# Two-input elementwise work moved to VectorE, small loads issued by GpSimd, conditioning chunks regrouped

## The chip, the cores and the metric

The kernel runs on one core of a Trainium2 chip. The metric is the device time of one execution in microseconds (us). Five engines work side by side, each with its own instruction queue that runs strictly in order: TensorE (PE in the profile) multiplies matrices, VectorE (DVE) and GpSimd (POOL) do elementwise work, ScalarE (ACT) applies functions of one input, SyncE (SP) issues most transfers. The transfers themselves run on 16 DMA engines. Semaphores tie the queues together.

## The reference

Two layers of a diffusion backbone work on 256 latent tokens and 256 context tokens of width 1024, in float32. Each layer first mixes tokens and then runs a mixture of experts:

```python
mod = silu(c) @ ada_w[l] + ada_b[l]          # 6 x 1024 values: shift, scale, gate, twice
h   = layer_norm(x) * (1 + scale) + shift
p   = h @ w_in                               # 1024 x 7328
branches = [mla(p), conformer_conv(p), fnet(p), rglru(p) * gelu(p)]
out = sum_k sigmoid(gate_k) * (branches[k] @ w_branch[k]) @ w_out
x   = layer_norm(alpha * x + gate * out)
x   = layer_norm(alpha * x + gate2 * expert_choice_moe(modulate(x)))
```

`rglru` is a gated linear recurrence in both directions. With r a sigmoid gate, log a = -8 softplus(-lambda) r, a = exp(log a), and the input is scaled by sqrt(1 - a^2). The conformer branch has a depthwise convolution with 31 taps. Layer 1 mixes only the latent tokens, with keys, values and recurrence states from the context.

## The kernel before

**Precision.** Products in the mixers are done with operands split in two parts: a high part, rounded by ScalarE (`S.activation(..., Copy)` into a 32-bit rounded type), and a low part, source minus high part (`lo_part`, line 148, one `tensor_tensor` subtraction). `mm3` (lines 151 to 153) then issues three matmuls: high by high, high by low, low by high. Every weight goes through `wsplit` (line 335), four 128 x 128 blocks at a time, into one of 4 (layer 0) or 5 (layer 1) pairs of buffers `wh`, `wl`. So each split costs one ScalarE and one subtraction, and TensorE can be some pairs ahead.

**Who subtracts.** `WSPLIT` deals the subtractions in turn: in layer 0 to GpSimd and VectorE alternately, in layer 1 three of five to GpSimd. GpSimd also has some other two-input operations: the square a*a of the recurrence (line 715), the sum of the two directions (line 734), the running sum over branches (line 496), and half of the low parts of `w_out` (line 1117).

**Order.** The mixer is written as code, and a scheduler in the language orders each engine's queue when the kernel is built. Convolution taps (line 525, 31 for each of four channel tiles, on VectorE) are queued in `later` and let out by `tick` four at a time (`PACE`) after each projection, so that they fill VectorE's gaps. The stages of a mixer are: four convolution inputs (glu), the Fourier branch, four recurrence tiles (`lru_in`, `lru_out`), attention; the gate and branch products of finished branches (`merge`) fill in between.

**Conditioning.** The 6144 columns of `ada_w` for each layer come in chunks. The first 2048 columns of layer 0 (shift and scale) are needed before anything else: `first_ada` loads eight chunks, each with 128 columns of shift and 128 of scale, as rows of 512 bytes. The other 27 chunks (384 columns, 1.5 MB each) sit in `ada_q`. `ada_more(AKEEP[l])` takes one at 24 places of a mixer while more than `AKEEP[l]` are left. A chunk takes a slot of the weight ring (three slots in the mixers), 8 small-output matmuls (`ada_mm`, line 208), one ScalarE copy, three transposes (line 218) and two small VectorE operations. With `AKEEP = (4, 0)`, 23 are done in layer 0's mixer, and the last four are loaded at its end (`AHELD`).

**Experts.** `finish` computes `w_out`, normalisation and routing, and then streams 16 experts' weights, 277 MB for each layer, through a ring.

Of the kernel before, what the change touches and what calls it, by code (L numbers as in the profile page):

```python
# [47 lines left out]
AKEEP = (4, 0)  # L48
AHELD = 4
WSPLIT = ("GV", "GGVGV")  # L50
# [49 lines left out]
def hybrid_kernel(ctx: ExitStack, tc: tile.TileContext, out: bass.AP, A):  # L100
# [102 lines left out]
    def ada_mm(l, pieces, w):  # L203
# [6 lines left out]
        part = adap[0].tile([128, 384], F32, name="adapart", tag="adapart", bufs=2)  # L210
        S.activation(out=part[:, 0:n], in_=ps[:, 0:n], func=AF.Copy)
        return l, pieces, part

    def ada_fin(l, pieces, part):
# [4 lines left out]
        red = const.tile([128, 3, 2], F32, name="adared", tag="adared", bufs=2)  # L219
# [53 lines left out]
    def params(l, rows):  # L273
# [29 lines left out]
        sp = const.tile([128, 4, 2, 2], F32, name="lsp", tag="lsp")  # L303
        V.tensor_tensor(out=p, in0=p, in1=mx, op=ALU.add)
        V.tensor_scalar(out=sp[:, :, :, 0], in0=p, scalar1=-4.0, scalar2=None, op0=ALU.mult)
        V.tensor_scalar(out=sp[:, :, :, 1], in0=p, scalar1=4.0, scalar2=None, op0=ALU.mult)
        prm[l, "sp"] = sp
# [10 lines left out]

    flip = [0]


    def mixer(l, tail=None):
# [12 lines left out]
        adap[0] = mixp  # L335
        def wsplit(v, k, m):
# [5 lines left out]
            flip[0] += 1  # L342
            lo_part(G if WSPLIT[l][flip[0] % len(WSPLIT[l])] == "G" else V, b, v, a)
# [9 lines left out]
        if both:  # L353
# [22 lines left out]
            params_load(0, rows, nc.scalar)  # L376
            parts = [ada_mm(*early.pop(0))]
            for j in range(KD):
                if j < 7:
                    parts.append(ada_mm(*(early.pop(0) if early else first_ada(j + 1))))  # L380
                ada_fin(*parts.pop(0))
# [20 lines left out]
        else:  # L402
# [4 lines left out]
            def front(t):  # L407
# [7 lines left out]
                for j0 in (0, 4):  # L415
# [12 lines left out]
                    lo_part(G if j0 else V, hl[:, j0:j0 + 4, c], hf[:, j0:j0 + 4], hh[:, j0:j0 + 4, c])  # L428
# [43 lines left out]
        def merge(b, br):  # L472
# [3 lines left out]
            for q in range(4):  # L476
# [7 lines left out]
                for i in range(2):  # L484
# [9 lines left out]
                    else:  # L494
                        V.scalar_tensor_tensor(out=sg, in0=sg, scalar=1.0, in1=pp[:, 0:N], op0=ALU.add, op1=ALU.mult)  # L495
                        G.tensor_tensor(out=merged[:, d, 0:N], in0=merged[:, d, 0:N], in1=sg, op=ALU.add)  # L496
# [78 lines left out]
        lo_part(G, dcl, dcf, dch)  # L575
        S.activation(out=dth, in_=dtf, func=AF.Copy)
        lo_part(G, dtl, dtf, dth)
# [84 lines left out]
        def lru_in(ct):  # L662
            bd = lp.tile([128, 2, 2, 128], F32, name="bd", bufs=nb2)
            G.memset(bd, 0.0)
            for ax, name in ((0, "lru_wa"), (1, "lru_wx")):
                for u in range(2):
                    nc.scalar.dma_start(out=bd[64 * u:64 * u + 64, :, ax, 64 * u:64 * u + 64],
                                        in_=A[name][l, :, 2 * ct + u].rearrange("d i j -> i d j"))
# [24 lines left out]
            lo_part(G, bl, bv, bh)  # L693
            return ge, xc, xh, xl, bh, bl

        def lru_out(ct, ge, xc, xh, xl, bh, bl):
# [13 lines left out]
            for d in range(2):  # L710
                a = lp.tile([128, 512], F32, name=f"a{d}", bufs=nb2)
                S.activation(out=a, in_=rr[d], func=AF.Exp, scale=sp[:, ct, d, 0:1], bias=sp[:, ct, d, 0:1])
                S.activation(out=rr[d], in_=rr[d], func=AF.Tanh, scale=sp[:, ct, d, 1:2], bias=sp[:, ct, d, 1:2])
                q = lp.tile([128, 512], F32, name="q2", bufs=2)
# [778 lines left out]
```

## Time and profile before

| what | value |
|---|---|
| median of 3 runs | 2454.8 us (2451.98 to 2458.52) |
| the profiled execution | 2450.92 us |
| its span in the trace | 2449.1 us |
| layer 0: mixer, then experts | about 0 to 620 us, then to 1362 us |
| layer 1: mixer, then experts | about 1362 to 1780 us, then to the end |

Times inside the trace are counted from the span's start; 1.8 us of the execution lie outside the span. An engine's busy time is the time in which at least one of its instructions runs; its share of a stretch says how full it was there, and the waits say who kept it from working. The granted clock is the share of TensorE's full speed in a stretch.

### The profile page before, as it was taken

The page shows a single profiled execution, that of the slowest core. Times are in us where ns is not written, and L with a number is a line of the kernel's source. Part 1 is how long each engine was busy: PE and PEld are TensorE (multiplying, and loading weights), DVE is VectorE, ACT ScalarE, POOL GpSimd, SP SyncE. Part 2 cuts the span into 40 slices and gives each one's busy share as a digit, 9 for nine tenths or more (in the row PEclk, how much of TensorE's full clock was granted, in tenths as well). Part 3 has the DMA queues.
Part 4 walks back from the last instruction along what each step waited for, and adds up shares of the span by engine and source line. Part 5 has one row for each costly group of instructions (what it writes and reads, how often), then busy time and mean ns, then how long its engine had stood idle before and what let it go on. Part 6 is the DMA issues. An engine that isn't in the chain of part 4 may idle for free.

```text
span 2449.1 us, 35574 instructions
## 1 busy us (share of the span) xinstructions
PE 2051.7 (84%) x14909; PEld 1212.6 (50%) x14909; DVE 983.3 (40%) x1811; ACT 632.4 (26%) x1162; POOL 394.8 (16%) x357
## 2 busy tenths in 40 slices
PE   6999999999879898898887788989967766767665
PEld 4876767757754343333332477778942211312111
DVE  5878844352671131121211688886551100100102
ACT  4354544452330010000000446656520000000000
POOL 1233322313300000000000155434600000000000
PEclk9999999999999999999999889999987666766658
DMA  9564444416579999999999443343699999999997
GB/s 273 163 183 148 155 119 138 135 34 230 166 288 395 423 420 422 423 423 423 423 423 423 148 119 116 87 139 104 222 375 423 423 423 424 423 423 423 424 423 302
DMA packets 238241, 713.11 MB, mean 291 GB/s; under 512 B 38183, under 2 KB 186137, under 8 KB 188928
## 3 DMA queue, kind: packets, MB, share of 16 engines
q1 hardware_dynamic: 227856, 703.37, 74.4%
q10 hardware_dynamic: 9072, 4.61, 0.7%
q8 instruction: 117, 1.92, 0.3%
q0 software_dynamic: 1152, 2.85, 0.3%
q14 instruction: 44, 0.36, 0.0%
HBM read 709.74 MB, written 1.05 MB: 290 GB/s over the span
## 4 chain that ended last, share of the span: by engine, by line
DMA 45%; PE 39%; DVE 7%; ACT 4%; issue 2%; POOL 1%; ACTq 0%; SPq 0%; DVEq 0%; POOLq 0%
DMA wslot<-in_w_e_down_dram 16%; DMA wslot<-in_w_e_up_dram 15%; DMA wslot<-in_w_e_gate_dram 13%; PE mm L151 6%; PE mm L153 6%; PE mm L152 6%; PE p L1348 3%; PE py L1386 2%; PE pp L153 2%; PE pp L151 2%; PE pp L152 2%; PE ax L208 2%; PE sc L909 1%; DVE conv L525 1%; PE xp L1229 1%
## 5 line engine op out<-in xcount | busy, mean ns | idle before, releaser
L1348 PE MATMUL p<-wslot,xe 128*32 128x352 f32 x6144 | 613.5, 544 | 164.4 <-DMA wslot<-in_w_e_gate_dram 94.5
L1348 PEld LDWEIGHTS p<-wslot,xe 128*32 128x32 f32 x6144 | 203.3, 122 | 561.2 <-issue 261.0
L1386 PE MATMUL py<-wslot,ht 128*32 128x256 f32 (+2 forms) x2176 | 283.0, 492 | 82.2 <-DMA wslot<-in_w_e_down_dram 42.2
L151 PE MATMUL mm<-hh,wh 128*128 128x512 f32 (+2 forms) x864 | 310.6, 360 | 11.7 <-ACT wh L341 4.9
L153 PE MATMUL mm<-hh,wl 128*128 128x512 f32 (+2 forms) x864 | 304.2, 353 | 17.3 <-DVE wl L148 13.4
L152 PE MATMUL mm<-hl,wh 128*128 128x512 f32 (+2 forms) x864 | 303.6, 352 | 0.4 <-DVE hl L148 0.4
L1361 DVE TENSOR_TENSOR he<-he,p 128x352 f32<-128x352 f32 x48 | 24.3, 507 | 683.1 <-PE p L1348 683.1
L148 POOL TENSOR_TENSOR wl<-wslot,wh 128x512 fp32r<-128x512 f32 (+1 forms) x163 | 225.4, 1389 | 417.8 <-ACT wh L341 394.0
L1360 ACT ACTIVATE he<-p 128x352 f32<-128x352 f32 x48 | 22.3, 464 | 964.7 <-PE p L1348 962.8
L341 ACT ACTIVATE wh<-wslot 128x512 fp32r<-128x512 f32 (+1 forms) x296 | 180.7, 624 | 288.6 <-PE mm L152 165.0
L1386 PEld LDWEIGHTS py<-wslot,ht 128*32 128x32 f32 (+1 forms) x2176 | 110.0, 130 | 248.7 <-issue 89.9
L1393 DVE SCALAR_TENSOR_TENSOR yt<-py,wix,gate 32x512 f32<-32x512 f32 (+1 forms) x128 | 78.6, 614 | 299.3 <-PE py L1386 297.8
L525 DVE SCALAR_TENSOR_TENSOR conv<-up,prm,conv 128x512 f32<-128x512 f32 (+1 forms) x240 | 194.2, 817 | 3.5
L151 PEld LDWEIGHTS mm<-hh,wh 128*128 128x128 f32 (+1 forms) x864 | 166.3, 193 | 49.0 <-issue 12.1
L153 PEld LDWEIGHTS mm<-hh,wl 128*128 128x128 f32 (+1 forms) x864 | 166.5, 193 | 43.1 <-DVE wl L148 15.7
L152 PEld LDWEIGHTS mm<-hl,wh 128*128 128x128 f32 (+1 forms) x864 | 166.7, 193 | 24.0 <-issue 3.1
L148 DVE TENSOR_TENSOR wl<-wslot,wh 128x512 fp32r<-128x512 f32 x133 | 109.5, 823 | 119.1 <-ACT wh L341 117.3
L153 PE MATMUL pp<-bh,wl 128*128 128x512 f32 (+1 forms) x256 | 87.2, 341 | 4.9 <-POOL wl L148 4.9
L151 PE MATMUL pp<-bh,wh 128*128 128x512 f32 (+1 forms) x256 | 87.3, 342 | 4.0 <-ACT bh L511 3.3
L152 PE MATMUL pp<-bl,wh 128*128 128x512 f32 (+1 forms) x256 | 86.7, 339 | 0.0
L1321 POOL DMA_DIRECT2D big<-in_ln_g_dram x1 | 0.6, 551 | 481.4 <-PE xp L1229 481.4
L496 POOL TENSOR_TENSOR big<-big,sg 128x512 f32<-128x512 f32 (+1 forms) x48 | 58.4, 1217 | 55.9 <-DVE sg L495 49.9
(367 smaller groups left out, 2569.9 us busy)
## 6 DMA issues: line engine op xcount, KB each, us to landing
wslot<-in_w_e_gate_dram SPq DMA_DIRECT2D x128, 1408.0 KB
wslot<-in_w_e_up_dram SPq DMA_DIRECT2D x128, 1408.0 KB
wslot<-in_w_e_down_dram SPq DMA_DIRECT2D x128, 1408.0 KB
wslot<-in_ada_w_dram SPq DMA_DIRECT2D x26, 1536.0 KB
wslot<-in_w_in_dram SPq DMA_DIRECT2D x36, 1024.0 KB
wslot<-in_w_branch_dram SPq DMA_DIRECT2D x32, 512.0 KB
wslot<-in_w_in_dram SPq DMA_DIRECT2D x30, 512.0 KB
wslot<-in_w_out_dram SPq DMA_DIRECT2D x12, 1024.0 KB
```

What stands on the lines that cost most here:

```text
L148: eng.tensor_tensor(out=lo, in0=src, in1=hi.bitcast(F32), op=ALU.subtract)
L151: T.matmul(o, lhsT=ah, rhs=bh, start=start, stop=False)
L152: T.matmul(o, lhsT=ah, rhs=bl, start=False, stop=False)
L153: T.matmul(o, lhsT=al, rhs=bh, start=False, stop=stop)
L208: T.matmul(ps[32 * g:32 * g + 32, 0:n], lhsT=csil[:, 2 * g + kk, :], rhs=w[:, 2 * g + kk, :], start=(kk == 0), stop=(kk == 1), skip_group_ ...
L341: S.activation(out=a, in_=v, func=AF.Copy)
L496: G.tensor_tensor(out=merged[:, d, 0:N], in0=merged[:, d, 0:N], in1=sg, op=ALU.add)
L525: V.scalar_tensor_tensor(out=cv, in0=up[:, :, k:k + 256], scalar=pm[:, ct, R_CVW + k:R_CVW + k + 1], in1=cv, op0=ALU.mult, op1=ALU.add)
L909: T.matmul(sc[:, 0:nk], lhsT=qt[:, q0:q0 + 128], rhs=kt[:, 0:nk], start=True, stop=True)
L1348: T.matmul(ts[si][32 * q:32 * q + 32, 0:FB], lhsT=xe[:, k, el, 32 * si:32 * si + 32], rhs=v[:, kk, FB * q:FB * q + FB], start=(k == 0), st ...
L1386: T.matmul(py[M * u:M * u + M, c:c + 256 * n], lhsT=ht[:, k], rhs=v[:, 256 * (i - 11 * kc):256 * (i - 11 * kc + n)], start=(k == 0), stop= ...
L1393: V.scalar_tensor_tensor(out=yt[s][32 * el:32 * el + 32, c], in0=py[ps_, 0:dw], scalar=wix[ps_, e:e + 1], in1=gate2[ps_, :], op0=ALU.mult, ...
```

## The change

Six edits go together.

1. `lo_part` runs on VectorE everywhere in the mixers and in `w_out`; so do the sum of the two directions and the running sum over branches. `WSPLIT` is gone.
2. The square of `a` becomes a second exponential on ScalarE, with twice the exponent (a third column of `sp`).
3. `params_load` of layer 0 (11 loads) and the block-diagonal gate weights `bd` (four loads for each of eight tiles) are issued by GpSimd instead of ScalarE; `bd` has one buffer in both layers.
4. The first eight conditioning chunks become four units of 256 shift and 256 scale columns, each loaded as two halves of the contraction, in rows of 1 KB (`first_ada`, `first_mm`); one unit serves two of the eight column tiles j.
5. `AKEEP` goes from (4, 0) to (11, 0): seven chunks pass from layer 0's mixer to layer 1's.
6. The inputs ctx and x are loaded as four transfers instead of two.

```diff
-AKEEP = (4, 0)
+AKEEP = (11, 0)
-WSPLIT = ("GV", "GGVGV")
...
+    def first_mm(u, pool):
+        ps = pax()
+        for half in range(2):
+            w = early.pop(0) if early else first_ada(2 * u + half)
+            for g in range(4):
+                T.matmul(ps[32 * g:32 * g + 32, :], lhsT=csil[:, 2 * g + half, :], rhs=w[:, g, :], start=(half == 0),
+                         stop=(half == 1), skip_group_check=True)
+        part = pool.tile([128, 512], F32, name="adafirst", bufs=2)
+        S.activation(out=part, in_=ps, func=AF.Copy)
+        return 0, [(256 * u, 256 * u + 256), (D + 256 * u, D + 256 * u + 256)], part
...
+        V.tensor_scalar(out=sp[:, :, :, 2], in0=p, scalar1=-8.0, scalar2=None, op0=ALU.mult)
...
-            flip[0] += 1
-            lo_part(G if WSPLIT[l][flip[0] % len(WSPLIT[l])] == "G" else V, b, v, a)
+            lo_part(V, b, v, a)
...
-            params_load(0, rows, nc.scalar)
-            parts = [ada_mm(*early.pop(0))]
+            params_load(0, rows, nc.gpsimd)
             for j in range(KD):
-                if j < 7:
-                    parts.append(ada_mm(*(early.pop(0) if early else first_ada(j + 1))))
-                ada_fin(*parts.pop(0))
+                if j % 2 == 0:
+                    ada_fin(*first_mm(j // 2, glp))
...
-                    lo_part(G if j0 else V, hl[:, j0:j0 + 4, c], hf[:, j0:j0 + 4], hh[:, j0:j0 + 4, c])
+                    lo_part(V, hl[:, j0:j0 + 4, c], hf[:, j0:j0 + 4], hh[:, j0:j0 + 4, c])
...
-                        G.tensor_tensor(out=merged[:, d, 0:N], in0=merged[:, d, 0:N], in1=sg, op=ALU.add)
+                        V.tensor_tensor(out=merged[:, d, 0:N], in0=merged[:, d, 0:N], in1=sg, op=ALU.add)
...
-            bd = lp.tile([128, 2, 2, 128], F32, name="bd", bufs=nb2)
+            bd = lp.tile([128, 2, 2, 128], F32, name="bd", bufs=1)
...
-                    nc.scalar.dma_start(out=bd[64 * u:64 * u + 64, :, ax, 64 * u:64 * u + 64],
+                    nc.gpsimd.dma_start(out=bd[64 * u:64 * u + 64, :, ax, 64 * u:64 * u + 64],
...
+                q = lp.tile([128, 512], F32, name="q2", bufs=2)
+                S.activation(out=q, in_=rr[d], func=AF.Exp, scale=sp[:, ct, d, 2:3], bias=sp[:, ct, d, 2:3])
                 S.activation(out=rr[d], in_=rr[d], func=AF.Tanh, scale=sp[:, ct, d, 1:2], bias=sp[:, ct, d, 1:2])
-                q = lp.tile([128, 512], F32, name="q2", bufs=2)
-                G.tensor_tensor(out=q, in0=a, in1=a, op=ALU.mult)
...
-            G.tensor_tensor(out=hs[0][:, t0:512], in0=hs[0][:, t0:512], in1=hs[1][:, t0:512], op=ALU.add)
+            V.tensor_tensor(out=hs[0][:, t0:512], in0=hs[0][:, t0:512], in1=hs[1][:, t0:512], op=ALU.add)
...
-                    lo_part(V if k0 else G, wl[:, k:k + 2, :], src, wh[:, k:k + 2, :])
+                    lo_part(V, wl[:, k:k + 2, :], src, wh[:, k:k + 2, :])
...
-    def first_ada(j):
-        return ada_load(0, [(128 * j, 128 * j + 128), (D + 128 * j, D + 128 * j + 128)])
+    def first_ada(i):
+        u, half = i // 2, i % 2
+        v = slot()[:, 0:2048].rearrange("p (g n) -> p g n", g=4)
+        for i in range(2):
+            c = i * D + 256 * u
+            nc.sync.dma_start(out=v[:, :, 256 * i:256 * i + 256],
+                              in_=A["ada_w"][0, :, c:c + 256].rearrange("(g h p) n -> h p g n", h=2, p=128)[half])
+        return v
```

The edits move instructions at three places that matter below.

TensorE at the start of layer 0, before (`ax` are the conditioning products, `adapart` their copy, `big` the normalised tokens, `mm` the first convolution input):

```order
L208 MATMUL ax<-wslot,csil 32x256 x24
L218 MATMUL tp<-c_ident,adapart 128x128 x2
L386 MATMUL tp<-c_ident,big 128x128 x4
L218 MATMUL tp<-c_ident,adapart 128x128 x2
L208 MATMUL ax<-wslot,csil 32x256
L386 MATMUL tp<-c_ident,big 128x128 x4
L208 MATMUL ax<-wslot,csil 32x256 x7
L218 MATMUL tp<-c_ident,adapart 128x128 x2
L151 MATMUL mm<-hh,wh 128x512
```

The same place in the change:

```order
L218 MATMUL ax<-wslot,csil 32x512 x8
L228 MATMUL tp<-c_ident,adafirst 128x128 x4
L393 MATMUL tp<-c_ident,big 128x128 x8
L218 MATMUL ax<-wslot,csil 32x512 x8
L228 MATMUL tp<-c_ident,adafirst 128x128 x4
L393 MATMUL tp<-c_ident,big 128x128 x8
L150 MATMUL mm<-hh,wh 128x512
L151 MATMUL mm<-hl,wh 128x512
```

Three eighths of the conditioning came before the first transposes of the tokens, one eighth at a time after; now it comes in quarters, and each quarter is followed by the transposes of two tiles instead of one.

VectorE at the end of `lru_out` of the first recurrence tile in layer 0, before (`q` is the scaled input, `r` holds the scans' results, `ge` the output, `wl` a weight's low part):

```order
L726 SCALAR_TENSOR_TENSOR r_1664<-a_1684,q_1687 128x512
L729 SCALAR_TENSOR_TENSOR r_1676<-a_1690,q_1693 128x256
L680 TENSOR_SCALAR xc<-xp,prm 128x512
L731 SCALAR_TENSOR_TENSOR r_1676<-a_1690,r_1676,q_1693 128x256
L683 SCALAR_TENSOR_TENSOR xc<-xp,prm,xc 128x512
L735 TENSOR_TENSOR ge<-ge,r_1664 128x512
L683 SCALAR_TENSOR_TENSOR xc<-xp,prm,xc 128x512
L148 TENSOR_TENSOR wl<-wslot,wh 128x512
L148 TENSOR_TENSOR bl<-ge,bh 128x512
```

The same place in the change:

```order
L736 SCALAR_TENSOR_TENSOR r_1615<-a_1629,q_1631 128x256
L687 TENSOR_SCALAR xc<-xp,prm 128x512
L738 SCALAR_TENSOR_TENSOR r_1615<-a_1629,r_1615,q_1631 128x256
L690 SCALAR_TENSOR_TENSOR xc<-xp,prm,xc 128x512
L741 TENSOR_TENSOR r_1603<-r_1603,r_1615 128x512
L690 SCALAR_TENSOR_TENSOR xc<-xp,prm,xc 128x512
L742 TENSOR_TENSOR ge<-ge,r_1603 128x512
L690 SCALAR_TENSOR_TENSOR xc<-xp,prm,xc 128x512
L231 TENSOR_REDUCE adared<-tp 128x6
L147 TENSOR_TENSOR bl<-ge,bh 128x512
L237 TENSOR_TENSOR mods_112<-adared,adab_108 128x6
L147 TENSOR_TENSOR wl<-wslot,wh 128x512 x2
```

The sum of the two scans (L741) now stands in VectorE's own queue, and the next low parts of weights stand behind it and behind the output `ge` and its low part `bl`, where before one stood ahead of `bl` and others were on GpSimd's queue.

SyncE's loads for layer 1's mixer from its first convolution input on, before:

```order
L134 DMA wslot<-in_w_in_dram 128x8x128 x8
L568 DMA wslot<-k_dftc_dram 128x256
L569 DMA wslot<-k_dftt_dram 128x2x256
L134 DMA wslot<-in_w_in_dram 128x8x256 x2
L134 DMA wslot<-in_w_in_dram 128x8x128 x4
L481 DMA wslot<-in_w_in_dram 128x8x256
```

The same place in the change:

```order
L133 DMA wslot<-in_w_in_dram 128x8x128 x4
L133 DMA wslot<-in_ada_w_dram 128x8x384
L133 DMA wslot<-in_w_in_dram 128x8x128 x2
L133 DMA wslot<-in_ada_w_dram 128x8x384
L133 DMA wslot<-in_w_in_dram 128x8x128 x2
L133 DMA wslot<-in_ada_w_dram 128x8x384
L575 DMA wslot<-k_dftc_dram 128x256
L576 DMA wslot<-k_dftt_dram 128x2x256
L133 DMA wslot<-in_w_in_dram 128x8x256 x2
L133 DMA wslot<-in_ada_w_dram 128x8x384 x2
L133 DMA wslot<-in_w_in_dram 128x8x128 x4
L488 DMA wslot<-in_w_in_dram 128x8x256
```

Five of the seven late conditioning chunks now stand between the convolution and Fourier weights, in the same three slots; the other two follow in the recurrence stage.

## Rows read from the trace of the kernel before

**Rows 1.** The page: the chain that ended last, by engine

```profile
DMA 45%; PE 39%; DVE 7%; ACT 4%; issue 2%; POOL 1%; ACTq 0%; SPq 0%; DVEq 0%; POOLq 0%
```

**Rows 2.** Windows by stage: stretch, length, busy (instructions) per engine, granted clock, DMA share, GB/s

```profile
0.00:62.00 62.00, 43.03 (x275) 27.76 (x276) 36.56 (x117) 29.38 (x51) 7.62 (x17) 1.00 1.01 274
...
130.00:320.00 190.00, 177.36 (x843) 133.27 (x842) 150.72 (x201) 95.24 (x149) 65.13 (x54) 0.98 0.48 150
320.00:620.00 300.00, 296.45 (x1405) 214.63 (x1405) 117.85 (x255) 133.25 (x265) 79.16 (x63) 1.00 0.42 133
800.00:1300.00 500.00, 433.90 (x4012) 178.22 (x4008) 99.80 (x191) 25.83 (x53) 6.54 (x13) 0.99 1.01 422
1400.00:1460.00 60.00, 47.14 (x313) 43.39 (x312) 52.04 (x85) 30.75 (x56) 27.46 (x24) 0.89 0.45 123
1460.00:1560.00 100.00, 83.69 (x514) 74.46 (x513) 78.17 (x95) 72.71 (x115) 50.16 (x43) 0.94 0.36 106
1560.00:1640.00 80.00, 71.22 (x407) 57.28 (x406) 71.18 (x123) 42.80 (x86) 33.52 (x28) 0.92 0.42 113
```

**Rows 3.** Windows: DMA with 512-byte runs, then 1-KB runs; TensorE in time, start

```profile
20.00:39.00 19.00, 15.30 (x106) 9.03 (x110) 9.61 (x29) 9.86 (x20) 2.58 (x2) 1.00 1.09 267
...
380.00:384.00 4.00, 4.00 (x19) 3.27 (x19) 0.56 (x1) 1.86 (x4) 1.28 (x1) 1.00 1.01 339
...
44.85 1.07 PE L208 MATMUL ax<-wslot,csil 128*32 128x256 f32 x16
63.21 1.50 PE L208 MATMUL ax<-wslot,csil 128*32 128x384 f32 x16
```

**Rows 4.** TensorE in order of time around one later conditioning chunk, layer 0

```profile
568.69 0.39 PE L153 MATMUL pp<-bh,wl 128*128 128x512 f32 x1
569.01 1.50 PE L208 MATMUL ax<-wslot,csil 128*32 128x384 f32 x16
570.44 0.50 PE L151 MATMUL mm<-hh,wh 128*128 128x512 f32 x1
...
571.26 0.49 PE L218 MATMUL tp<-c_ident,adapart 128*128 128x128 f32 x3
```

**Rows 5.** Line 148 on DVE, then POOL; taps by form; taps in time; GpSimd's low parts

```profile
130.00:320.00 190.00, 26.74 (x35) 43.50 (x30) 0.98 0.48 150
1360.00:1640.00 280.00, 52.56 (x63) 100.10 (x71) 0.91 0.40 111
...
L525 DVE SCALAR_TENSOR_TENSOR conv<-up,prm,conv 128x256 f32<-128x256 f32 x110 | 76.3, 708 | 1.2
...
1438.15 2.85 DVE L525 SCALAR_TENSOR_TENSOR conv<-up,prm,conv 128x256 f32<-128x256 f32 x7
...
L148 POOL TENSOR_TENSOR wl<-wslot,wh x163: 459/1294/1904, 48.3 to 1758.6; 128x512 fp32r<-128x512 f32 x161, 128x128 fp32r<-128x128 f32 x2
```

**Rows 6.** End of one recurrence gate in layer 0, GpSimd and VectorE; exponential by form

```profile
184.68 1.64 POOL L734 TENSOR_TENSOR r<-r,r 128x512 f32<-128x512 f32 x1 [4.50 <-DVE r L731]
...
188.69 0.68 DVE L148 TENSOR_TENSOR wl<-wslot,wh 128x512 fp32r<-128x512 f32 x1
...
L712 ACT ACTIVATE a<-r,lsp 128x512 f32<-128x512 f32 x16 | 12.9, 813 | 0.1
```

**Rows 7.** TensorE waits in 130:320, 1400:1560 and 620:735: total, times, longest

```profile
PE mm L153 <- DVE wl L148: 5.7, 3, 2.7
...
PE mm L153 <- DVE wl L148: 7.7, 3, 3.1
...
PE mm L153 <- POOL wl L148: 2.7, 3, 1.1
...
PE wo L1120 <- POOL wol L148: 3.0, 4, 1.0
```

**Rows 8.** ScalarE at the block-diagonal loads; GpSimd issuing one small load

```profile
149.68 0.63 ACT L341 ACTIVATE wh<-wslot 128x512 fp32r<-128x512 f32 x1 [4.16 <-POOL bd L664]
...
856.45 0.52 POOL L266 DMA_DIRECT2D he<-in_cv_b_dram  x1 [176.88 <-DVE he L264]
```

More of the change, by code (lines that the diff above doesn't have):

```diff
@@ L209, in ada_mm @@
                          start=(kk == 0), stop=(kk == 1), skip_group_check=True)
-        part = adap[0].tile([128, 384], F32, name="adapart", tag="adapart", bufs=2)
+        part = adap[0].tile([128, 384], F32, name="adapart", tag="adapart", bufs=adab["bufs"])
         S.activation(out=part[:, 0:n], in_=ps[:, 0:n], func=AF.Copy)
         return l, pieces, part
+    def first_mm(u, pool):
[8 more added lines that the diff above has]
+        return 0, [(256 * u, 256 * u + 256), (D + 256 * u, D + 256 * u + 256)], part
     def ada_fin(l, pieces, part):
@@ L218, in ada_fin @@
             T.transpose(tp[:, 128 * i:128 * i + 128], part[:, 128 * i:128 * i + 128], ident)
-        red = const.tile([128, 3, 2], F32, name="adared", tag="adared", bufs=2)
+        red = const.tile([128, 4, 2], F32, name="adared", tag="adared", bufs=2)
         m = n // 128
@@ L302, in params @@
         V.tensor_scalar(out=mx, in0=lam, scalar1=-1.0, scalar2=0.0, op0=ALU.mult, op1=ALU.max)
-        sp = const.tile([128, 4, 2, 2], F32, name="lsp", tag="lsp")
+        sp = const.tile([128, 4, 2, 3], F32, name="lsp", tag="lsp")
         V.tensor_tensor(out=p, in0=p, in1=mx, op=ALU.add)
@@ L317, in ada_more @@
             ada_chunk(*ada_q.pop(0))
-    flip = [0]
     def mixer(l, tail=None):
@@ L335, in mixer @@
         adap[0] = mixp
+        adab["bufs"] = 2 if both else 1
         def wsplit(v, k, m):
@@ L574, in mixer @@
         S.activation(out=dch, in_=dcf, func=AF.Copy)
-        lo_part(G, dcl, dcf, dch)
+        lo_part(V, dcl, dcf, dch)
         S.activation(out=dth, in_=dtf, func=AF.Copy)
-        lo_part(G, dtl, dtf, dth)
+        lo_part(V, dtl, dtf, dth)
         nt = N // 128
@@ L692, in lru_in @@
             S.activation(out=bh, in_=bv, func=AF.Copy)
-            lo_part(G, bl, bv, bh)
+            lo_part(V, bl, bv, bh)
             return ge, xc, xh, xl, bh, bl
@@ L1261, in finish @@
         wpx.close()
+        adab["bufs"] = 2
         adap[0] = lnx.enter_context(tc.tile_pool(name=f"adp{l}", bufs=1, side="left", reuse_waits="tile"))
@@ L1451, in hybrid_kernel @@
     for s, name in ((0, "ctx"), (1, "x")):
-        nc.sync.dma_start(out=big[:, 2 * s:2 * s + 2, :], in_=A[name][0].rearrange("(t p) d -> p t d", p=128))
+        for t in range(2):
+            nc.sync.dma_start(out=big[:, 2 * s + t, :], in_=A[name][0, 128 * t:128 * t + 128, :])
     early = [first_ada(j) for j in range(3)]
```

## Prediction

> **What bounds the kernel now.** I read the chain of waits first: it ends with DMA at 45% and TensorE at 39% [rows 1]. The windows say where each of the two rules [rows 2]. In the experts' stages (800 to 1300 us) the DMA engines are full, share 1.01 at 422 GB/s: nothing in this change touches them, and time won or lost in a mixer moves everything behind it one to one. From 320 to 620 us, layer 0's mixer is TensorE alone: busy 296.45 of 300 us at clock 1.00. From 130 to 320 us it is busy 177.36 of 190, so 13 us are waits. Layer 1's mixer is different: from 1400 to 1640 us TensorE is busy 47.14 + 83.69 + 71.22 = 202 of 240 us and VectorE 52.04 + 78.17 + 71.18 = 201, at a granted clock of 0.89 to 0.94. Two engines at 84% each means that they wait for each other. GpSimd has 111 us of work there.
>
> **The change part by part.** The sum is made against the profiled execution, 2450.9 us (span 2449.1 and 1.8 outside it); the median of the runs shown, 2454.8, lies 3.9 above it.
>
> *First conditioning units (edit 4), and the inputs in four loads (edit 6).* Eight chunks of 1.05 MB, 8.39 MB in all, must land before the first weights are used, and the DMA is full through the first 62 us, share 1.01 [rows 2]. Between 20 and 39 us, when the loads are of this form, the DMA share is 1.09 at 267 GB/s; where a later chunk with longer rows loads alone, it is 1.01 at 339 GB/s [rows 3]. So the queue is full both times and only the row length differs that I can see. 8.39 MB take 31.4 us at 267 and 24.7 us at 339: -6.7. TensorE takes the last early chunk at 44.85 us, the first later one at 63.21 [rows 3]; now a unit stands behind two half loads, and what follows the last one is two tiles and not one, which gives back under 1 us. I take -6; bounds -8 (the whole and a little of the input loads) and 0. By the Trainium skill ("DMA: Bandwidth & Descriptors", the property table at its head) transfers of 512 B and more already run at line rate. By that rule the regrouping would give nothing; the two rates in the rows speak against it, though they are of different stretches. It is the second rival below.
>
> *Seven chunks leave layer 0 (edit 5).* A chunk there costs TensorE 1.43 us from its first product at 569.01 to the next projection product at 570.44, and 0.49 us for the transposes [rows 4]: 1.9 us. The stretch is full, so 7 x 1.9 = 13 us go: -13 (bounds -14 and -7, if half of them now open onto another wait). Their loads go too, off a queue with share 0.42, which gives nothing.
>
> *They arrive in layer 1.* The same 13 us of products into a stretch with 240 - 202 = 38 us of TensorE idle. Each chunk is 1.57 MB, at 339 GB/s 4.6 us on the queue of SyncE, and stands in the same three slots as the projection weights; five of seven come between the convolution and Fourier weights. What is queued behind a late chunk there is the next weights, and for them TensorE. With DMA at 0.36 to 0.45 there is room for 7 x 4.6 = 32 us of loads. Two products in three fall into idle time: +5. Bounds 0 and +14.
>
> *Low parts on VectorE in layer 1 (edit 1).* From 1360 to 1640 us 71 subtractions ran on GpSimd in 100.10 us, 1.41 each, and 63 on VectorE in 52.56, 0.83 each [rows 5]. The moved ones cost VectorE what one costs undisturbed, 0.68 [rows 6]: 71 x 0.68 = 48 us, with the running sums and the sums of directions some 52. But what GpSimd did slowed VectorE: 110 convolution taps of 128x256 took 0.708 us on the mean, and seven in a row with nothing beside them 2.85 us, 0.41 each [rows 5]. If GpSimd falls silent, 110 x 0.30 = 33 us and 63 x 0.15 = 9 come back. VectorE ends near 10 us above where it stood, still below TensorE's length with the chunks. What TensorE waited for: 7.7 us on VectorE's and 2.7 on GpSimd's low parts between 1400 and 1560 [rows 7]. A low part now needs 0.68 in place of 1.41 us, but behind other work in one queue. I take -8, near those 10.4 us, because taps shortened by 42% are what a low part stands behind; bounds -20 (half of the 38 idle us) and +5.
>
> *Recurrence in layer 0 (edits 1 and 2).* The sum of directions took GpSimd 1.64 us at the end of the chain, after a wait of 4.50 for the scan [rows 6]; VectorE does it in about 0.7. The square leaves GpSimd, estimated at the 1.41 us of a subtraction of that size there, and comes back as an exponential of 0.813 us for each direction on ScalarE [rows 6], which is busy 95 of 190 us [rows 2]. At this place in the order of after, the next weights' low parts stand behind the sum, `ge` and `bl`, about 2 us of VectorE work; four pairs of buffers cover that, at three products of about 0.4 us in each of four blocks. Net -3 from 5.7 us of waits on VectorE's low parts [rows 7]; bounds -6 and +6.
>
> *w_out (edit 1).* TensorE waited 3.0 us for GpSimd's `wol` in layer 0 [rows 7]: -2 of it, and -2 taken alike at the end of layer 1. Bounds -6 and +2 together, since 24 more subtractions now share one queue.
>
> *Small loads (edit 3).* ScalarE stood 4.16 us behind the block-diagonal loads, whose buffer GpSimd had to clear [rows 8]; this lies in the -3 above. GpSimd issues one small load in 0.52 us [rows 8]; 32 of them in two mixers lie where it has nothing else to do. With one `bd` buffer in layer 1 the next clearing waits for the split of the tile before, which lies a whole tile earlier in ScalarE's queue: 0. By the Trainium skill ("SBUF — State Buffer", SBUF: two separate sides) descriptors of loads issued by GpSimd are not written while certain VectorE instructions hold the port that the two share, which would make such loads late. By that rule the 4.16 us would stay and the -3 become about 0. No row here shows such a load late, nor tests it.
>
> Sum: -6 - 13 + 5 - 8 - 3 - 2 - 2 = -29, so 2450.9 - 29 = 2422 for an execution like the profiled one, and with the 3.9 us to the median **2426 us**. All times below have the 3.9 in them.
>
> **The rivals.**
>
> *Boot does not shorten.* If 267 GB/s came from the start of the kernel (many queues, inputs and conditioning together) and not from the row length, the -6 is 0: 2432. For it: the two rates come from different stretches. Against it: share 1.09 shows the engines full, so packets were dear, not missing.
>
> *VectorE becomes the single feeder (slower).* Every low part of a weight now goes through one queue in order, with taps, scans and normalisation ahead of it; 163 weights' low parts move [rows 5]. TensorE's waits on VectorE's low parts were 5.7 us from 130 to 320 us, where it made 35 (0.16 each) [rows 5, 7], and 7.7 in 1400 to 1560. If the moved ones each bring 0.28 us of wait more than I count, that is 46 us: 2472. It decides from 29/163 = 0.18 us each, or nine waits of the longest seen, 3.1 us. For it: this is about the rate that VectorE's own low parts show already, and VectorE is at 84% in layer 1. Against it: between two of them stand at most three or four taps in the new order, 1.6 us at 0.41, and four to five pairs of buffers cover that; and layer 0's VectorE is busy only 118 of 300 us [rows 2].
>
> *Layer 1 is fed fully.* If the two engines were waiting for each other through GpSimd's slow subtractions, more than 10 us come back. TensorE's 202 us at full clock are 47.14 x 0.89 + 83.69 x 0.94 + 71.22 x 0.92 = 186, so 54 us of the 240 are idle or lost to the clock. Half of it is -27 in place of -8: 2407. Against it: clock and idle come together, and VectorE stays as full.
>
> *Late chunks stay exposed.* If three slots cannot hold a chunk and the next weights, half of the 4.6 us of each is seen, 3.5 x 4.6 = 16, and all of the 13 us instead of 5: +24, 2450. For it: five of them follow each other within one stage. Against it: the DMA is at 0.36 to 0.45, and in layer 0 the same ring carried 23 chunks with TensorE at 99%.
>
> **How the numbers follow.** Forecast 0.54, boot 0.12, fed fully 0.11, exposed 0.11, single feeder 0.12. A measurement of this kernel can tell about 0.3%, 7.4 us, from no change. The forecast, the boot case and the fed case are all beyond it on the fast side (0.77), and a third of the exposed case with them: faster 0.80. The exposed case's middle part is within it: same 0.08. The feeder case gives slower 0.12. The forecast's own range is 2410 to 2438, from the bounds of layer 1 and the recurrence taken together, which do not all fall on one side. The range that is left when the feeder case and some of the fed case are cut is 2398 to 2452.
>
> **What the changed profile would show.** Boot: the DMA moves above 300 GB/s between 20 and 39 us, and the last first-unit product starts near 39 us, not 45; at 45 the boot case holds. Layer 0: the full TensorE stretch is 13 us shorter, with clock 1.00. Layer 1: 128x256 taps near 0.42 us, low parts near 0.69, GpSimd nearly silent. TensorE's waits on VectorE's low parts below 10 us in 1400 to 1560 confirm the -8; 25 or more there, or in 130 to 320, show the single feeder. Waits on DMA of `wslot` of more than 10 us show exposed chunks. The forecast fails if taps stay at 0.7 us though GpSimd is silent, since then VectorE has 42 us more work than I count.

## The result, and the profile after

The changed kernel takes 2416.92 us (median, 2415.83 to 2418.24) against 2455.09 (2451.98 to 2458.52) for the kernel before: ratio 0.9847, 95% interval 0.9835 to 0.9858, so 38 us less. The forecast was 2426 us, 29 less. In the traces the spans differ by 34.4 us (2449.1 and 2414.7), since the traced run of the kernel before lies 4 us under its median.

Where it went is read from the starts of the same TensorE instructions in each trace (first `wo`, the first product of `w_out`, and last `p` of the experts), in us:

| stage | before | after | gain | forecast |
|---|---|---|---|---|
| span's start to first `wo` of layer 0 | 628.53 | 599.07 | 29.5 | 22 |
| from there to the last `p` of layer 0 | 722.57 | 721.57 | 1.0 | 2 |
| from there to first `wo` of layer 1 | 412.32 | 408.60 | 3.7 | 3 |
| rest | 685.72 | 685.47 | 0.2 | 2 |

The page of the changed kernel: busy time, share of the span and instructions by engine, and the chain that ended last, which answers to [rows 1]:

```profile
PE 2040.9 (85%) x14845; PEld 1211.7 (50%) x14845; DVE 1012.4 (42%) x2073; ACT 647.9 (27%) x1178; POOL 42.4 (2%) x112
```

```profile
DMA 49%; PE 38%; DVE 6%; ACT 6%; issue 1%; ACTq 0%; SPq 0%; DVEq 0%
```

GpSimd has left the chain. The windows that answer to [rows 2, 3], same columns:

```profile
130.00:320.00 190.00, 186.13 (x901) 138.96 (x900) 153.79 (x249) 110.37 (x171) 9.04 (x21) 1.00 0.50 153
320.00:620.00 300.00, 291.41 (x1350) 219.41 (x1349) 157.59 (x330) 132.64 (x267) 2.30 (x5) 0.99 0.35 110
20.00:39.00 19.00, 17.55 (x94) 9.92 (x93) 11.41 (x43) 9.11 (x16) 0.98 (x2) 1.00 1.02 297
```

From 130 to 320 us TensorE is now busy 186 of 190 us, where it was 177; from 20 to 39 us the loads move 297 GB/s and not 267. The forms on VectorE in layer 1's mixer, as busy us and mean ns of one, after (between 1330 and 1610 us):

```profile
L147 DVE TENSOR_TENSOR wl<-wslot,wh 128x512 fp32r<-128x512 f32 x98 | 66.0, 682 | 13.9 <-ACT wh L351 13.6
L532 DVE SCALAR_TENSOR_TENSOR conv<-up,prm,conv 128x256 f32<-128x256 f32 x115 | 54.0, 475 | 0.3
```

and the low part before (between 1360 and 1640 us), which took longer for the same operation:

```profile
L148 DVE TENSOR_TENSOR wl<-wslot,wh 128x512 fp32r<-128x512 f32 x37 | 35.8, 968 | 8.8 <-ACT wh L341 8.6
```

The taps fell from 708 ns [rows 5] to 475, a low part from 968 to 682. VectorE did 61 more of these low parts there. Over the whole of layer 1's mixer, from the last `p` of layer 0 to the first `wo` of layer 1, it was busy hardly longer, 316.68 us for 315.00, with 663 instructions in place of 513 (before, then after, columns as in [rows 2]):

```profile
1351.10:1763.40 412.30, 356.38 (x2276) 301.26 (x2269) 315.00 (x513) 238.45 (x443) 187.60 (x169) 0.94 0.42 122
1320.64:1729.24 408.60, 365.90 (x2409) 303.64 (x2402) 316.68 (x663) 252.88 (x462) 14.21 (x41) 0.95 0.51 152
```

### The profile page after: what moved, and what is told of

The parts are those of the page before. It is cut to its first block, busy times and chain, and to the rows that moved or that the text cites. A ratio compares the mean times of both kernels' runs of the same rounds, so it can differ in the third digit from the quotient of the medians.

```text
span 2414.7 us, 35251 instructions
## 1 busy us (share of the span) xinstructions
PE 2040.9 (85%) x14845; PEld 1211.7 (50%) x14845; DVE 1012.4 (42%) x2073; ACT 647.9 (27%) x1178; POOL 42.4 (2%) x112
## 4 chain that ended last, share of the span: by engine, by line
DMA 49%; PE 38%; DVE 6%; ACT 6%; issue 1%; ACTq 0%; SPq 0%; DVEq 0%
DMA wslot<-in_w_e_down_dram 17%; DMA wslot<-in_w_e_up_dram 16%; DMA wslot<-in_w_e_gate_dram 15%; PE mm L150 6%; PE mm L152 6%; PE mm L151 6%; PE p L1356 2%; PE pp L152 2%; PE pp L150 2%; PE pp L151 2%; PE py L1394 1%; PE sc L916 1%; PE ax L207 1%; PE po L941 1%; PE wo L1127 1%
## 5 line engine op out<-in xcount | busy, mean ns | idle before, releaser
L1356 PE MATMUL p<-wslot,xe 128*32 128x352 f32 x6144 | 605.0, 538 | 165.8 <-DMA wslot<-in_w_e_gate_dram 90.9
L147 DVE TENSOR_TENSOR wl<-wslot,wh 128x512 fp32r<-128x512 f32 (+1 forms) x296 | 199.4, 680 | 120.1 <-ACT wh L351 116.1
L1394 PEld LDWEIGHTS py<-wslot,ht 128*32 128x32 f32 (+1 forms) x2176 | 115.3, 132 | 250.6 <-issue 95.1
L150 PEld LDWEIGHTS mm<-hh,wh 128*128 128x128 f32 (+1 forms) x864 | 163.5, 190 | 47.0 <-issue 10.4
L532 DVE SCALAR_TENSOR_TENSOR conv<-up,prm,conv 128x512 f32<-128x512 f32 (+1 forms) x240 | 145.9, 611 | 1.7
L1244 ACT ACTIVATE xe<-xp,mp 128x128 f32<-128x128 f32 x48 | 22.0, 458 | 176.7 <-PE xp L1236 96.2
L1127 PE MATMUL wo<-wol,mh 128*128 128x256 f32 x192 | 55.5, 289 | 3.2 <-DVE wol L147 2.8
L1125 PE MATMUL wo<-woh,mh 128*128 128x256 f32 x192 | 55.8, 292 | 0.0
```

Source lines behind the costliest of these rows:

```text
L147: eng.tensor_tensor(out=lo, in0=src, in1=hi.bitcast(F32), op=ALU.subtract)
L150: T.matmul(o, lhsT=ah, rhs=bh, start=start, stop=False)
L532: V.scalar_tensor_tensor(out=cv, in0=up[:, :, k:k + 256], scalar=pm[:, ct, R_CVW + k:R_CVW + k + 1], in1=cv, op0=ALU.mult, op1=ALU.add)
L1125: T.matmul(o, lhsT=mh[:, k0 + k, tt], rhs=wh[:, k, :], start=(k0 + k == 0 and i == 0), stop=False, skip_group_check=True)
L1127: T.matmul(o, lhsT=mh[:, k0 + k, tt], rhs=wl[:, k, :], start=False, stop=False, skip_group_check=True)
L1356: T.matmul(ts[si][32 * q:32 * q + 32, 0:FB], lhsT=xe[:, k, el, 32 * si:32 * si + 32], rhs=v[:, kk, FB * q:FB * q + FB], start=(k == 0), st ...
```

## The experiments

Two theories were at stake. The first: VectorE was slowed by what GpSimd did beside it, and taking GpSimd's elementwise work away is what pays, most of it in layer 1. The rival: the gain is TensorE's shorter list of work in layer 0 (late chunks, boot), and VectorE's queue gains and loses about as much. Differences between single kernels below carry the intervals of their ratios, some 3 us each.

**Edit 1 alone, put into the kernel before** (o1_vector):

```diff
-WSPLIT = ("GV", "GGVGV")
+WSPLIT = ("V", "V")
-            G.tensor_tensor(out=hs[0][:, t0:512], ...
+            V.tensor_tensor(out=hs[0][:, t0:512], ...
```

(and the other lines of edit 1 alike)

> The kernel before with edit 1 alone. Theory (edit 1 stands by itself): 2455 - 16 = 2439 us, taps of 128x256 at 0.42 us on the mean in layer 1. Rival of the prediction (VectorE as the single feeder): 2455 or more, with more waits for VectorE's low parts than the 13 us of before. Second rival (edit 1 pays only together with the chunks in layer 1): 2450 to 2455.

2422.18 us, ratio 0.9860 (0.9843 to 0.9877): 33 us less from this edit alone (28.8 between the traces), twice what even the theory expected. Layer 0 up to its `wo` gains 10.2 us, layer 1 up to its `wo` 19.1 (412.32 to 393.25). Taps take 477 ns here. The single feeder and the second rival both fall by the time. The largest group of TensorE's waits on VectorE's low parts in this kernel's layer 1 (us, times, longest) is about what [rows 7] had, 7.7:

```profile
PE mm L153 <- DVE wl L148: 8.2, 6, 3.6
```

**Edit 1 undone, the rest kept** (u1_split; the diff is that of edit 1, backwards).

> The change without its first edit: low parts dealt to GpSimd and VectorE as before, sum of directions, running sum and w_out's halves on GpSimd again; all else as changed. Theory (edit 1 carries what boot and chunks do not, since VectorE loses its 102 us of slowing beside GpSimd): the 9 us of waits in layer 0's recurrence and some 9 in layer 1 come back, 2435 us. Rival (the recurrence waits went by the exponential and the loads, edits 2 and 3): at most +8, 2425 us.

2465.68 us, ratio 1.0044 (1.0031 to 1.0058): not 18 but 49 us slower than the whole change, and slower than the kernel before. Without edit 1 the other five lose. In layer 1 this kernel needs 440.22 us to `wo`, before 412.32, and taps take 626 ns on the mean. That the late chunks meet a slowed VectorE there is a reading: no run takes the chunks out of this kernel, which also has the second exponential.

**GpSimd's load put back, with no result that anyone uses** (d2_two, and d1_one with one input). In layer 1, three weight pairs of five:

```diff
+                for c in range(0, k * m, 256):
+                    n = min(256, k * m - c)
+                    h = wh[:, c:c + n].bitcast(F32)
+                    G.tensor_tensor(out=dum[:, 0:n], in0=h, in1=h, op=ALU.subtract)
```

and in d1_one the last line is

```diff
+                    G.tensor_scalar(out=dum[:, 0:n], in0=h, scalar1=1.0, scalar2=None, op0=ALU.mult)
```

> The change, and in layer 1 GpSimd also does a two-input subtraction for three of five weight pairs, as it did before, on the high part alone and into a tile that no one reads (in pieces of 256 columns). No one waits for it, so what it costs is the slowing of VectorE. Theory (slowing by GpSimd is what the change removed in layer 1): taps of 128x256 rise from about 0.42 to 0.6 us or more, and the time by 8 to 16 us, 2425 to 2433. Rival (the gain was the wait for GpSimd's slow results): 2417 to 2419 us, even if taps get slower.

> The same with a one-input multiplication by 1 on GpSimd in place of the subtraction. Theory (only two-input work on GpSimd slows VectorE's two-input work): taps stay near 0.42 us, 2417 to 2419 us. Rival, by the Trainium skill (SBUF - State Buffer, two separate sides: the lock holds against any GpSimd operation that reads that memory): taps and time rise about as with two inputs, 2423 to 2433 us.

Two inputs: 2447.63 us (ratio 0.9974, 0.9964 to 0.9984), 31 us slower than the change, more than the theory's 8 to 16. One input: 2423.81 (0.9874, 0.9853 to 0.9895), 7 slower. Layer 1 up to its `wo` in d2_two, then in d1_one:

```profile
1320.25:1760.02 439.77, 376.22 (x2409) 310.59 (x2402) 364.38 (x663) 253.20 (x462) 168.64 (x231) 0.93 0.47 140
1321.33:1737.61 416.28, 368.30 (x2409) 304.92 (x2402) 332.46 (x663) 252.74 (x462) 212.80 (x231) 0.95 0.49 147
```

VectorE has the same 663 instructions in both and in the change, and was busy 316.68 us in the change, 332.46 with one-input and 364.38 with two-input work beside it. Layer 1 of d2_two, 439.77 us, is as long as that of u1_split. GpSimd's form and the taps in d2_two:

```profile
L363 POOL TENSOR_TENSOR dum<-wh 128x256 f32<-128x256 f32 x152 | 126.3, 831 | 226.6 <-ACT wh L356 218.9
```

```profile
L543 DVE SCALAR_TENSOR_TENSOR conv<-up,prm,conv 128x256 f32<-128x256 f32 x117 | 64.6, 557 | 0.3
```

and the same two in d1_one:

```profile
L363 POOL TENSOR_SCALAR dum<-wh 128x256 f32<-128x256 f32 x168 | 179.2, 1067 | 171.0 <-ACT wh L356 161.0
```

```profile
L543 DVE SCALAR_TENSOR_TENSOR conv<-up,prm,conv 128x256 f32<-128x256 f32 x120 | 60.5, 509 | 0.3
```

Line 543 is the taps' line in these kernels. GpSimd was busy longer with one input (179 us against 126), and yet slowed the taps less: from 475 ns to 509, with two inputs to 557. So the slowing is real, costs time though no one reads GpSimd's result, and depends on the form. A two-input form also reads twice as much, and the runs do not tell the number of inputs from the amount read. Of d1_one's expectations neither holds whole: the taps did not stay near 0.42 us, as the theory had it, and they rose far less than with two inputs, though the time lies in the rival's range. One thing is not clean: ScalarE waited for the tile that GpSimd still read, 4.5 us in d2_two and 5.1 in d1_one. As that is alike in both, the 24 us between them are not from it; of d1_one's 7 us it may be the greater part.

**The late chunks undone** (u5_chunks).

```diff
-AKEEP = (11, 0)
+AKEEP = (4, 0)
```

> The change with AKEEP back at (4, 0), so that the seven chunks are done in layer 0 again. Theory (layer 0's mixer is TensorE alone, layer 1's has idle TensorE time beside a full VectorE): the seven cost 2.08 us each there, as the stretches of the two traces differ (14.6 us for seven), and free about 2 us in layer 1: 2417 + 13 = 2430 us. Rival (a chunk costs TensorE as much in layer 1 as in layer 0): 2417 to 2420 us.

2421.14 us, ratio 0.9861 (0.9846 to 0.9876): only 4 us slower than the change. The start to `wo` of layer 0 is 14.1 us longer (613.12), as the theory had it, but layer 1 is 12.6 us shorter (395.98 against 408.60), which neither theory priced right: nearer to the rival. The stretch between them is 2.8 us longer. The place shows in the trace of the change. ScalarE's waits between 1375 and 1435 us, then 10 us of that stretch, columns as in [rows 2]:

```profile
ACT wh L351 <- DMA wslot<-in_w_in_dram: 9.7, 4, 4.9
```

```profile
1395.00:1405.00 10.00, 5.41 (x27) 4.88 (x26) 7.09 (x18) 3.45 (x6) 0.00 (x0) 0.75 1.05 335
```

The DMA is full, ScalarE waits for projection weights behind chunks in the ring, TensorE works 5.41 of 10 us and its granted clock falls to 0.75. That chunk loads stay exposed was a rival of the prediction. Its sign was more than 10 us of waits on DMA of `wslot`, no engine named. ScalarE's 9.7 us lie at that mark (0.7 in u5_chunks between 1375 and 1475); TensorE itself waited 1.4 us for a chunk.

**The chunks moved on within layer 1** (s_spread), past the convolution and the Fourier branch:

```diff
-            if ct:
+            if ct and both:
                 ada_more(AKEEP[l])
...
-        ada_more(AKEEP[l])
+        if both:
+            ada_more(AKEEP[l])
```

(the last twice, in the Fourier branch)

> The change, but in layer 1 no conditioning chunk between the convolution and the Fourier weights: the places there are skipped, so that the seven late chunks fall to the gates and the recurrence behind. Theory (five loads in one stage, 1.5 MB each, fill the DMA and keep ScalarE waiting 9.7 us for projection weights; the recurrence has idle TensorE time and half-empty DMA): of the 12.6 us that the chunks cost layer 1, 5 to 8 come back, 2409 to 2412 us. Rival (a chunk costs TensorE and the ring as much anywhere in layer 1): 2416 to 2419 us.

2406.53 us, ratio 0.9801 (0.9788 to 0.9815): 10 us faster than the change. Layer 1 takes 399.25 us to `wo`; seven chunks now cost it 3.3 us and not 12.6. ScalarE's wait for projection weights in the same stretch:

```profile
ACT wh L351 <- DMA wslot<-in_w_in_dram: 2.1, 1, 2.1
```

So it is the place of the chunks, not the amount of TensorE's work on them, that cost the 9 us. Layer 1 up to its `wo` in s_spread, then in u5_chunks:

```profile
1322.18:1721.43 399.25, 358.95 (x2409) 299.21 (x2402) 316.65 (x663) 255.41 (x464) 14.22 (x41) 0.97 0.52 156
1337.50:1733.48 395.98, 349.62 (x2276) 296.87 (x2269) 313.86 (x649) 249.52 (x455) 14.27 (x41) 0.95 0.44 128
```

Against the change, TensorE is 7.0 us less busy in s_spread with the same 2409 instructions (358.95 for 365.90), at a granted clock of 0.97 for 0.95, and 2.4 us less idle. The products moved with their loads: that the loads are what counted is read from ScalarE's wait, 7.6 us shorter, and not tested apart from the idle time that the products find in the recurrence.

**The square back on GpSimd** (u2_square).

```diff
-                q = lp.tile([128, 512], F32, name="q2", bufs=2)
-                S.activation(out=q, in_=rr[d], func=AF.Exp, scale=sp[:, ct, d, 2:3], bias=sp[:, ct, d, 2:3])
                 S.activation(out=rr[d], in_=rr[d], func=AF.Tanh, ...
+                q = lp.tile([128, 512], F32, name="q2", bufs=2)
+                G.tensor_tensor(out=q, in0=a, in1=a, op=ALU.mult)
```

> The change with the square on GpSimd again. Theory (the chain of a gate gets about 0.5 us longer for each of 16 squares, and half of them are waited for, 3 to 4 us; beside that a two-input operation on GpSimd slows VectorE a little): 2421 us. Rival (it is off the path): 2417 us.

2409.58 us, ratio 0.9816 (0.9797 to 0.9834): 7 us faster than the change; both expectations fell. Layer 0 is the same (599.16 us to `wo`), layer 1 6.6 us shorter (401.99). The chain of one recurrence tile in layer 1 on ScalarE after, in order of time (start, us, engine, line):

```profile
1523.34 0.80 ACT L719 ACTIVATE a<-r,lsp 128x512 f32<-128x512 f32 x1
...
1524.78 0.80 ACT L721 ACTIVATE q<-r,lsp 128x512 f32<-128x512 f32 x1
1525.48 0.80 ACT L719 ACTIVATE a<-r,lsp 128x512 f32<-128x512 f32 x1
1526.19 0.80 ACT L722 ACTIVATE r<-r,lsp 128x512 f32<-128x512 f32 x1
1526.89 0.80 ACT L721 ACTIVATE q<-r,lsp 128x512 f32<-128x512 f32 x1
...
1528.12 0.80 ACT L722 ACTIVATE r<-r,lsp 128x512 f32<-128x512 f32 x1
1528.94 1.28 ACT L728 ACT_TABLE_LOAD   x1
```

and with the square on GpSimd, ScalarE and then GpSimd:

```profile
1518.47 0.80 ACT L719 ACTIVATE a<-r,lsp 128x512 f32<-128x512 f32 x1
...
1519.93 0.80 ACT L720 ACTIVATE r<-r,lsp 128x512 f32<-128x512 f32 x1
1520.63 0.80 ACT L719 ACTIVATE a<-r,lsp 128x512 f32<-128x512 f32 x1
...
1521.86 0.80 ACT L720 ACTIVATE r<-r,lsp 128x512 f32<-128x512 f32 x1
1522.68 1.28 ACT L728 ACT_TABLE_LOAD   x1
```

```profile
1521.51 1.04 POOL L722 TENSOR_TENSOR q<-a 128x512 f32<-128x512 f32 x1 [1.12 <-ACT a L719]
```

From the first `a` to the table load are 5.60 us with six functions of `r` and 4.21 with four: two exponentials of 0.80 more in one queue, where GpSimd's 1.04 lay beside the next function. Four tiles by 1.4 us would be 5.6 of the 6.6 us. That layer 0 loses nothing fits TensorE having other products to do there; no run tests it.

**The small loads back on ScalarE** (u3_loads).

```diff
-            params_load(0, rows, nc.gpsimd)
+            params_load(0, rows, nc.scalar)
-                    nc.gpsimd.dma_start(out=bd[64 * u:64 * u + 64, ...
+                    nc.scalar.dma_start(out=bd[64 * u:64 * u + 64, ...
```

> The change with the small loads (11 parameter loads, block-diagonal weights) issued by ScalarE again, one buffer for the block-diagonal weights. Theory (ScalarE stands behind them for about 4 us a few times, and about half of that is waited for): 2421 us. Rival (no one waits): 2417 us. A second rival, by the Trainium skill (SBUF - State Buffer, two separate sides): loads issued by GpSimd can be held up by VectorE, and then this kernel is the faster one, 2414 us.

2424.66 us, ratio 0.9882 (0.9864 to 0.9901): 8 us slower than the change, twice the theory's figure. Layer 0 to its `wo` is 6.4 us longer. More than half of it is there at the start already: the ninety-seventh projection product starts at 66.04 us, in the change at 62.25. The first copy of a conditioning product on ScalarE in the change, then in u3_loads, with the end of the product and the last two load issues ahead of it:

```profile
18.96 0.60 ACT L221 ACTIVATE adafirst<-ax 128x512 f32<-128x512 f32 x1 [2.05 <-PE ax L218]
```

```profile
16.44 1.94 PE L218 MATMUL ax<-wslot,csil 128*32 128x512 f32 x8 [1.08 <-DMA wslot<-in_ada_w_dram]
...
21.06 0.23 ACTq L280 DMA_DIRECT2D rows<-in_q_norm_g_dram  x1
25.73 0.23 ACTq L281 DMA_DIRECT2D rows<-in_kv_norm_g_dram  x1
26.00 1.09 ACT L221 ACTIVATE adafirst<-ax 128x512 f32<-128x512 f32 x2 [9.11 <-DMA rows<-in_lru_ba_dram]
```

The product ends at 18.38 us, the last of eleven load issues starts on ScalarE's queue at 25.73, and the copy behind it at 26.00, after 9.11 us in which ScalarE did no work. The issues themselves are short, 0.23 us here; the queue stands between them, and the profile names the landing of earlier small loads as what it waited for. SyncE's next load stood in the same way, and the DMA engines were not full in that time, with a share of 0.72 (SyncE's wait, then the window, both in u3_loads):

```profile
SPq L370 <- DMA rows<-in_cv_w_dram: 5.4, 1, 5.4
...
16.90:26.00 9.10, 5.34 (x24) 0.43 (x16) 0.00 (x0) 0.00 (x0) 0.00 (x0) 1.00 0.72 217
```

Why the queue waited so long for these landings no run shows. The kernel before had such a wait too:

```profile
24.92 0.23 ACTq L271 DMA_DIRECT2D rows<-in_kv_norm_g_dram  x1
25.20 0.66 ACT L211 ACTIVATE adapart<-ax 128x256 f32<-128x256 f32 x2 [5.11 <-DMA rows<-in_q_norm_g_dram]
```

By the Trainium skill ("SBUF — State Buffer", SBUF: two separate sides) loads issued by GpSimd can be held up while VectorE holds the port that the two share. The kernel with these loads on GpSimd is the faster one, so such a delay, if there was any, cost less than the loads gained. The eleven loads at the start do not test it, since VectorE was busy only 0.56 of 6 us while most of them were issued:

```profile
14.00:20.00 6.00, 4.21 (x18) 0.77 (x19) 0.56 (x4) 3.27 (x5) 4.27 (x9) 1.00 1.10 332
```

**The early chunks as before** (u4_boot).

```diff
+            parts = [ada_mm(*early.pop(0))]
...
-                if j % 2 == 0:
-                    ada_fin(*first_mm(j // 2, glp))
+                if j < 7:
+                    parts.append(ada_mm(*(early.pop(0) if early else first_ada(j + 1))))
+                ada_fin(*parts.pop(0))
```

> The change with the eight early chunks of 128 + 128 columns (rows of 512 bytes) again, the inputs still in four loads. Theory (TensorE, not the DMA, is what is full from 26 us on in either form, so that only the earlier first convolution product counts): +2.4 us, 2419. Rival (the loads set the pace and the predicted 6 us are there, but lost behind): the start of the mixer is 6 us later, 2423 us.

2414.80 us, ratio 0.9835 (0.9821 to 0.9848): no difference from the change that these intervals tell, and both expectations were too high. Its ninety-seventh projection product starts at 62.62 us, the change's at 62.25, that of before at 64.64. So the regrouping is worth about 0.4 us at this point and nothing that shows in the time; the rest of the 2.4 came with other edits. The small loads make 3.8 us there with the regrouped start (u3_loads) and 0.7 with the old one (64.19 in o1_vector, 63.47 in o13_vec_loads); the inputs in four loads have no run of their own.

**Edits 1 and 3 alone** (o13_vec_loads, o1_vector with the lines of u3_loads the other way).

> The kernel before with edits 1 and 3 alone (elementwise work on VectorE, small loads by GpSimd); square, early chunks, inputs and AKEEP as before. Theory (single edits add: 2422 with edit 1, and the loads are worth some 8, so that exponential, regrouping and late chunks bring nothing together): 2413 to 2416 us. Rival (the loads are worth something only with the regrouped start): 2420 to 2422 us.

2415.54 us, ratio 0.9838 (0.9825 to 0.9852): the same as all six edits. The other four bring nothing together, which fits the chunks' gain of 4 us (u5_chunks) beside the exponential's loss of 7 (u2_square). The change also gives `adapart` one buffer in place of two in layer 1's mixer, which the list of edits leaves out; no run has that alone.

**A version that beats both** (s_spread_sq and s_spread14_sq): the change with chunks as in s_spread and the square on GpSimd; the second has `AKEEP = (14, 0)` besides.

> The same with the square on GpSimd again. Theory (the two add, the square is worth 6.5 us in layer 1's recurrence): 2403 to 2406 us. Rival (chunks in the recurrence stand in the way of the chain that the square shortens, or fill what it leaves idle): 2409 us, as with the square alone.

> The same with AKEEP at (14, 0), three more chunks in layer 1. Theory (layer 0 gives 2.08 us for each, layer 1's recurrence takes under 1 us for each as long as it has idle time): 3 to 4 us under the kernel with eleven, 2400 to 2402 us. Rival (idle time is used up, each costs 1.8 us in layer 1 as on the mean of the seven): the same time within 1 us.

2399.21 us (ratio 0.9769, 0.9755 to 0.9782) and 2395.19 (0.9755, 0.9742 to 0.9768). Both lie below what was expected. The gains add: 18 us under the change for the two, and 4 for three chunks more, which take 5.4 us from layer 0 and give layer 1 1.9.

## Why the prediction came out as it did

The time lay in the range and the sign was right, and the mechanism behind the largest gain was the one that was argued. But five terms were off by 5 us or more, and the sum came near by errors that cancel: that is luck.

*Low parts on VectorE in layer 1, -8*: the step that was mis-sized most. Alone it is worth 19 us in layer 1 (o1_vector), and beside the other five 32 (u1_split, 440.22 to 408.60), beyond its bound of -20. The mechanism was as argued, GpSimd slowing VectorE (d2_two). The price was taken from the 10.4 us that TensorE waited for low parts, and more than these waits came back. Layer 1 in o1_vector:

```profile
1341.29:1734.54 393.25, 350.55 (x2276) 297.86 (x2269) 316.11 (x649) 244.62 (x447) 13.05 (x33) 0.96 0.45 131
```

Of the 19 us, 13 are idle time of TensorE (42.7 for 55.9 us), and 6 are its work: 350.55 us for 356.38 with the same 2276 instructions, at a granted clock of 0.96 for 0.94. The prediction gave a price for the clock only in its rival "fed fully". "VectorE ends near 10 us above where it stood" was off as well. In windows of 280 us from the same place it ended 5 lower (233.26 before from 1360, 228.67 after from 1330). Taps gave back 26 us (110 by 0.23), not 33. But weights' low parts alone gave 11 (37 by 0.29), where the prediction had 9 for all low parts, and the recurrence, which it left out, gave more: `xc` fell from 1002 to 742 ns, the scaling of `q` from 969 to 692.

*The late chunks in layer 1, +5*: 12.6, within the bound of +14. The step that failed is "Two products in three fall into idle time". TensorE's busy time grew by 16.3 us against u5_chunks (349.62 to 365.90), and its idle time fell only from 46.4 to 42.7. Where the chunks stand in s_spread, busy time grew by 9.3 and idle time fell by 6.1, which is two thirds; 9 us went with that move. The rival "exposed" had these loads ahead of the weights, at 24 us.

*Seven chunks leave layer 0, -13*: 14.1, right.

*First units, -6*: 0.4 (u4_boot). "So the queue is full both times" took the DMA for the bound of the start. TensorE was busy without a break there, 6.00 of 6.00 us, between 39 and 45 us of the kernel before:

```profile
39.00:45.00 6.00, 6.00 (x56) 3.96 (x52) 5.24 (x32) 2.53 (x5) 0.00 (x0) 1.00 1.21 290
```

Convolution products stood between the conditioning products, so faster loads had little to shorten. In the change the last early product starts at 43.22 us, not near 39. That longer rows move faster is borne out all the same: between 20 and 39 us u4_boot, which differs from the change in this form alone, moved 271 GB/s with rows of 512 bytes, the change 297 with rows of 1 KB, at a smaller share.

```profile
20.00:39.00 19.00, 14.74 (x122) 9.31 (x118) 13.38 (x52) 10.66 (x20) 1.48 (x3) 1.00 1.11 271
```

The Trainium skill ("DMA: Bandwidth & Descriptors", Specifications) gives 512 bytes as the least transfer for line rate; these two rates do not agree with it. The gain was worth next to nothing here. The rival "boot does not shorten" was right, for another reason than it gave. The 339 GB/s, which the prediction took for a conditioning chunk alone, belong to other loads: just before that window SyncE issued weights of a gate and of a branch, and the next chunk only at 388.60 us.

```profile
377.70 0.38 SPq L481 DMA_DIRECT2D wslot<-in_w_in_dram  x1
378.13 0.57 SPq L482 DMA_DIRECT2D wslot<-in_w_branch_dram  x1
...
388.60 0.37 SPq L134 DMA_DIRECT2D wslot<-in_ada_w_dram  x1
```

*Small loads, "lies in the -3"*: some 8 us by themselves (u3_loads; o1_vector against o13_vec_loads 6.6). The row of ScalarE's wait of 4.16 us [rows 8] was read, but the same was not asked of the start, where ScalarE's queue stood among the eleven issues.

*Recurrence and w_out in layer 0, -5*: edit 1 alone took 10 us up to the end of `w_out`, nearly all before it. The exponential is a loss of 6 to 7 us in layer 1, where the prediction counted its +0.81 for layer 0 only. The square that it replaces took GpSimd 1.04 us (u2_square), not the 1.41 of the estimate.

*Single feeder*: it would have shown 25 us of TensorE's waits on VectorE's low parts or more in one stretch; between 1370 and 1526 us of the change there were

```profile
PE mm L152 <- DVE wl L147: 5.7, 2, 3.6
```

and 0.6 us more, where [rows 7] had 7.7 and 2.7. Fewer than 10 us were to confirm the -8. They came, and the step was worth more than twice as much: the sign does not tell its size.

## What to carry to other kernels

Price two engines' elementwise work together: what moves off GpSimd can cost VectorE next to nothing in sum (315.00 and 316.68 us here), since VectorE's own operations get shorter; look for one form with two durations. When work is moved to a place with idle compute, check what its load stands in front of in the ring there. And an in-order engine that also issues loads is held by what these issues wait for; read its first useful instruction's wait, not its busy share.

## What was not expected of the hardware

GpSimd's two-input work slowed VectorE's taps more than its one-input work, though the one-input work kept GpSimd busy 179 us and the other 126: 557 against 509 ns, 475 with GpSimd nearly silent. With eleven small loads in its queue ScalarE did no work for 9.11 us at the start, while the DMA engines had a share of 0.72. And TensorE's granted clock fell to 0.75 in the ten microseconds of layer 1 in which ScalarE waited for projection weights and TensorE was busy 5.41 of 10; there are other such dips, 0.78 between 1490 and 1500 us with 5.30 of 10 us busy.
